# Two token tiles of a recurrence block share one matmul, ScalarE gathers the keys, and the output weights move into the mixer's weight buffers

## The chip, the cores and the metric

The kernel runs on one core of a Trainium2 chip. The metric is the device time of one launch in microseconds (us). The engines are TensorE (PE, with its weight loads as PEld), VectorE (DVE), ScalarE (ACT), GpSimd (POOL) and SyncE (SP), which issues most of the DMAs.

## The reference, cut to what matters

One layer of a hybrid encoder works on x, 2048 tokens of width 1024, in float32:

- A mixer: x += W_out [ DiffAttn(4 heads) || HGRN2(4 heads) ] (W_in RMSNorm(x)). The attention is causal by chunks of 64 tokens and takes the difference of two softmaxes. HGRN2 is a gated linear recurrence with 128 key and 128 value channels per head: within a chunk of 64 tokens, `att[t,s] = sum_k q[t,k] k[s,k] exp(b[t,k] - b[s,k])` for s <= t, where b is the running sum of the logarithms of the forget gates, and `o[t] = sum_s att[t,s] v[s] + (q exp(b)) state`; the state is carried from chunk to chunk.
- A feed-forward part: x += W_down (silu(conv3(u)) * v), with u and v from W_up RMSNorm(x).

## The kernel before, in words

The mixer runs over four heads `s`, and in a head over eight blocks `b` of 256 tokens, which are two token tiles of 128. For each head it loads the columns of W_in that the head needs, split into a high and a low half that are multiplied in three matmuls: `WA` (query, key, value of the attention), `WB` (value and gate of HGRN2), `WC` (query and forget gate of HGRN2). In a block, a string of letters gives the order in which the steps are written: projections (`A`, `B`, `I`, `J`, `C`) and transposes (`t`, `u`) of the next block, attention of this one (`a`, `b`, `x`, `y`), `h` for the recurrence within the block (`hgrn`), `k` for its output and state (`hgrn_o`). A compile-time scheduler turns what is written into one fixed queue for each engine; it mixes the steps by priority and by its own estimate of durations, and places all semaphores. Each engine works its queue off in order.

`hgrn` computes the matrix `att` of a tile in seven levels, h = 1, 2, 4, ... 64. At level h, the tokens are cut into runs of h; a run on the right side of a pair takes queries, the run on its left takes keys. For each of the block's two tiles one matmul (L441) multiplies the keys `kS` of the tile (128 - h columns as weights) with the 64 queries `qP` of the right-hand runs, and a masked copy (L444) on VectorE puts the result into the tile's `att`. Then VectorE multiplies the right-hand queries and the left-hand keys by the decay `T` of the neighbouring run (L449, L450) and shortens `T` by half (L452). The products of both tiles are made in one instruction. An f32 matmul shows as two records in the trace. `lt`, the result in PSUM, has one buffer, which it shares with `op` and `sp` of `hgrn_o`. `hgrn_o` multiplies `att` with the values, adds the part of the state, and renews the state (`sp`, L477).

The last stage of the first half, the output projection, holds W_out in eight tiles `wo`, of 128 rows each, with a high and a low half. Each is loaded to a buffer `raw`, cast by ScalarE (L537), and the low half is subtracted by GpSimd for even tiles and by VectorE for odd ones (L538). `wo` belongs to a pool that is opened after the mixer's pools are closed. For each token tile, `load_o` reads the mixer's output, transposes it on TensorE and splits it into `oT` (L555, L556); 48 matmuls `pjo` (L599 to L601) follow, and the residual, norm and transposes for the feed-forward part. That part (L619 on) isn't touched by the diff.

Of the kernel before, what the change touches and what calls it, by code (L numbers as in the profile page):

```python
# [18 lines left out]
P = 128  # L19
D = 1024  # L20
S = 2048
# [3 lines left out]
ROW = 512  # L25
TOP, FEW, SMALL, SMALL2 = 480, 192, 320, 192
FF = 2816
# [32 lines left out]


@with_exitstack
def hymba_kernel(ctx, tc, x, ln1_w, w_in, q_norm_w, k_norm_w, lam_q1, lam_k1, lam_q2, lam_k2,
                 diff_subln_w, hgrn_lb_logits, hgrn_norm_w, w_out, ln2_w, w_up, conv_w, conv_b,
                 w_down, out):
    nc = tc.nc
# [50 lines left out]
    hgw = cst.tile([P, P], F32, name="hgw")  # L117
    lmask = few.tile([P, 7, 64], U8, name="lmask")
    NATT = 3
    atts = [cst.tile([P, P], F32, name=f"att{n}") for n in range(NATT)]  # L120

# [13 lines left out]
    def load_rest(tmp, tmq):  # L135
        lamv = tmp[:, 0:256].rearrange("p (n e) -> p n e", n=4)
        lbd = tmp[:, 256:268].rearrange("p (n e) -> p n e", n=3)
        lmf = tmq[:, 0:448].rearrange("p (l e) -> p l e", l=7)
        for hf in range(2):
# [32 lines left out]
        POOL.tensor_copy(out=lmask, in_=lmf)  # L172
        for a in atts:
            POOL.memset(a, 0.0)
# [8 lines left out]


    with ExitStack() as ms:
        wp = pool(ms, "wp", 1)
        kv = pool(ms, "kv", KVB, side="right")
# [25 lines left out]
        def phase1(b):  # L213
# [42 lines left out]
        for s in range(4):  # L256
# [87 lines left out]
            def attn(b, j):  # L344
# [9 lines left out]
                for si, (k0, k1) in enumerate(segs):  # L354
                    for c in range(2):
# [71 lines left out]
            def hgrn(b):  # L427
                f, kS, qP, qk = HG.pop(b)
                T = f
                TT = wk.tile([P, BLK], F32, name="TT", tag="TT", bufs=FB)  # L430
                to = 0
                att = [atts[(2 * b + g) % NATT] for g in range(2)]
                for li, h in enumerate(LEVELS):
                    nb = BLK // (2 * h)
                    nk = P - h
                    lt = ps.tile([P, 2, 64], F32, name="lt", tag=HT, bufs=HB)
                    qv = qP.rearrange("p (n two h) -> p n two h", two=2, h=h)
                    kvw = kS.rearrange("p (n two h) -> p n two h", two=2, h=h)
# [9 lines left out]
                    Tv = T.rearrange("p (n two) -> p n two", two=2)  # L448
                    DVE.tensor_tensor(out=qv[:, :, 1, :], in0=qv[:, :, 1, :], in1=Tv[:, :, 0:1].broadcast_to([P, nb, h]), op=ALU.mult)  # L449
                    DVE.tensor_tensor(out=kvw[:, :, 0, :], in0=kvw[:, :, 0, :], in1=Tv[:, :, 1:2].broadcast_to([P, nb, h]), op=ALU.mult)  # L450
                    Tn = TT[:, to:to + nb]
                    DVE.tensor_tensor(out=Tn, in0=Tv[:, :, 0], in1=Tv[:, :, 1], op=ALU.mult)  # L452
                    T = Tn
                    to += nb
                HG[b] = (qk, kS, qP, T)

            def hgrn_o(b):
                qk, kS, qP, T = HG.pop(b)
                att = [atts[(2 * b + g) % NATT] for g in range(2)]
                for g in range(2):  # L460
# [61 lines left out]
    up_st = ExitStack()  # L522
    hp = pool(up_st, "hp3", 1, side="right")
    with ExitStack() as ms:
        wp = pool(ms, "wp2", 1)
# [5 lines left out]
        pa = pool(ms, "pa2", 2, space=PSUM, side="right")  # L531
        WO = []
        for kt in range(ND):
            raw = rw.tile([P, D], F32, name="raw", tag="raw")
            dma(out=raw, in_=w_out[kt * P:(kt + 1) * P, :])
            w = wp.tile([P, 2, D], F32R, name=f"wo{kt}")
            ACT.copy(w[:, 0], raw)  # L537
            (POOL if kt in WOP else DVE).tensor_tensor(out=w[:, 1], in0=raw, in1=w[:, 0].bitcast(F32), op=ALU.subtract)  # L538
            WO.append(w)

        OT = {}

        def load_o(i):
            ot = wk.tile([P, D], F32, name="ot", tag="ot")
            dma(out=ot, in_=o_d[i])
            xt = wk.tile([P, D], F32, name="xt", tag="xt", bufs=XTB)
            dma(out=xt, in_=x[i * P:(i + 1) * P, :])
            oT = [wk.tile([P, D], F32R, name="oT", tag=f"oT{a}", bufs=2) for a in range(2)]
            for hf in range(2):
                tp = pa.tile([P, 512], F32, name="tpo", tag="x")  # L550
                for q in range(4):
                    kt = hf * 4 + q
                    PE.transpose(tp[:, q * P:(q + 1) * P], ot[:, kt * P:(kt + 1) * P], ident)
                cs = slice(hf * 512, hf * 512 + 512)
                ACT.copy(oT[0][:, cs], tp)  # L555
                DVE.tensor_tensor(out=oT[1][:, cs], in0=tp, in1=oT[0][:, cs].bitcast(F32), op=ALU.subtract)  # L556
            OT[i] = (oT, xt)
# [319 lines left out]
HT, HB = "h", 1  # L877
WOP = (0, 2, 4, 6)
EARLY, TP, LO, HSB, HVB, XTB = 1, 1, 2, 5, 3, 2
LOPOOL = (6,)  # L880
# [28 lines left out]
```

## Time and profile before

| | us |
|---|---|
| median of 3 runs | 2762.63 |
| lowest and highest run | 2759.31, 2767.03 |
| the profiled execution | 2761.66 |
| its span in the trace | 2760.0 |
| PE busy | 2662.2 (96%) |
| DVE busy | 1892.9 (69%) |
| ACT busy | 1212.4 (44%) |
| POOL busy | 1053.6 (38%) |

The span is that of the profiled execution; busy times are sums of the instructions' durations without overlap within an engine. Matmuls are pipelined, so the duration of one is longer than what it takes of the queue: that is read from the distance of the starts.

### The profile page before, as it was taken

To read this page: it belongs to the slowest core of one execution; us is meant where nothing else is said; L and a number is where in the kernel's file an instruction comes from. 1 tells how busy PE (TensorE), PEld (TensorE's weight loads), DVE (VectorE), ACT (ScalarE), POOL (GpSimd) and SP (SyncE) were. 2 spreads that over 40 slices of the span, in tenths; PEclk is the share of its full clock that TensorE was granted. 3 is DMA by queue.
4 is the path that set the end of the run, shared out by engine and by line. 5 is a ranking of instruction groups with operands and counts; after the bars stand their busy time and mean duration, and the time that the engine had idled before them with its cause. 6 is when DMAs were issued, how large, how long until landed. Compare 5 with 4: busy or idle time off the path is not lost. (4 is left out here: it accounts for less than half of the span.)

```text
span 2760.0 us, 43193 instructions
## 1 busy us (share of the span) xinstructions
PE 2662.2 (96%) x15170; PEld 2329.6 (84%) x15170; DVE 1892.9 (69%) x4051; ACT 1212.4 (44%) x2878; POOL 1053.6 (38%) x1153
## 2 busy tenths in 40 slices
PE   7999999999999999989999999999999998899999
PEld 6888999999999999978877888887888886687887
DVE  4667855676667666773338666668777768978787
ACT  4555544454345444454335344345434434334332
POOL 2222222212222222220334443444344347877775
PEclk9999999999999999999999999999999999999999
DMA  5333422232222322125754232225222234775754
GB/s 183 119 109 112 130 89 86 82 124 83 99 83 75 115 91 84 50 88 172 248 192 142 83 92 75 86 92 175 77 85 91 70 92 129 170 159 132 178 172 168
DMA packets 273494, 322.96 MB, mean 117 GB/s; under 512 B 19470, under 2 KB 238974, under 8 KB 269182
## 3 DMA queue, kind: packets, MB, share of 16 engines
q1 hardware_dynamic: 266366, 295.04, 32.8%
q0 software_dynamic: 6912, 25.17, 5.3%
q8 instruction: 120, 1.97, 0.3%
q14 instruction: 96, 0.79, 0.1%
HBM read 198.50 MB, written 104.86 MB: 110 GB/s over the span
## 5 line engine op out<-in xcount | busy, mean ns | idle before, releaser
L684 PE MATMUL q<-xT,WS 128*128 128x512 f32 x704 | 274.4, 390 | 2.4 <-DVE xT L617 2.4
L683 PE MATMUL q<-xT,WS 128*128 128x512 f32 x704 | 274.4, 390 | 0.5 <-ACT xT L616 0.5
L685 PE MATMUL q<-xT,WS 128*128 128x512 f32 x704 | 274.3, 390 | 0.6 <-DVE WS L617 0.4
L797 PE MATMUL pd<-TW,SG 128*128 128x512 f32 x616 | 245.1, 399 | 21.2 <-DVE acc L803 7.1
L799 PE MATMUL pd<-TW,SG 128*128 128x512 f32 x616 | 243.2, 396 | 2.2 <-DVE SG L617 2.2
L798 PE MATMUL pd<-TW,SG 128*128 128x512 f32 x616 | 244.0, 397 | 0.5 <-DVE TW L617 0.5
L616 ACT CAST WS<-st 128x512 fp32r<-128x512 f32 x176 | 108.4, 618 | 243.6 <-PE q L685 227.1
L684 PE MATMUL q<-xB,WS 128*128 128x512 f32 x528 | 205.9, 390 | 2.2 <-DVE xB L617 2.2
L685 PE MATMUL q<-xB,WS 128*128 128x512 f32 x528 | 206.1, 390 | 1.2 <-DVE WS L617 1.2
L683 PE MATMUL q<-xB,WS 128*128 128x512 f32 x528 | 205.8, 390 | 0.7 <-ACT xB L616 0.7
L378 ACT ACTIVATE p<-sc,nm 128x1024 f32<-128x1024 f32 (+4 forms) x192 | 165.7, 863 | 90.3 <-DVE nm L367 87.5
L617 POOL TENSOR_TENSOR WS<-st,WS 128x512 fp32r<-128x512 f32 x44 | 88.2, 2004 | 278.4 <-ACT WS L616 258.8
L252 PE MATMUL pj<-WA,hT 128*128 128x384 f32 x512 | 176.4, 344 | 4.1 <-DVE hT L239 4.1
L367 DVE TENSOR_REDUCE nm<-sc 128x1 f32<-128x1024 f32 (+4 forms) x192 | 174.5, 909 | 6.9 <-PE sc L363 4.3
L253 PE MATMUL pj<-WA,hT 128*128 128x384 f32 x512 | 175.3, 342 | 0.0
L254 PE MATMUL pj<-WA,hT 128*128 128x384 f32 x512 | 174.5, 341 | 0.0
L797 PEld LDWEIGHTS pd<-TW,SG 128*128 128x128 f32 x616 | 118.1, 192 | 52.1 <-DVE acc L803 7.6
L684 PEld LDWEIGHTS q<-xT,WS 128*128 128x128 f32 x704 | 132.3, 188 | 30.4 <-DVE xT L617 3.1
L685 PEld LDWEIGHTS q<-xT,WS 128*128 128x128 f32 x704 | 132.3, 188 | 29.0 <-DVE WS L617 1.4
L683 PEld LDWEIGHTS q<-xT,WS 128*128 128x128 f32 x704 | 132.4, 188 | 28.6 <-ACT xT L616 0.9
L616 ACT CAST WS<-rawu 128x512 fp32r<-128x512 f32 x132 | 82.0, 623 | 159.2 <-PE q L685 159.2
L252 PE MATMUL pjc<-hT,WC 128*128 128x256 f32 x512 | 151.6, 296 | 0.2 <-ACT ig L321 0.2
(412 smaller groups left out, 7857.3 us busy)
## 6 DMA issues: line engine op xcount, KB each, us to landing
hT<-hTd SPq DMA_DIRECT2D x24, 2048.0 KB, 7.9
rawu<-in_w_up_dram SPq DMA_DIRECT2D x176, 256.0 KB, 3.1
x2d<-acc POOLq DMA_DIRECT2D x48, 512.0 KB, 6.5
gd<-c SPq DMA_DIRECT2D x176, 128.0 KB, 1.8
G<-gd SPq DMA_DIRECT2D x24, 768.0 KB, 4.2
xt<-in_x_dram SPq DMA_DIRECT2D x32, 512.0 KB, 4.1
hTd<-hT SPq DMA_DIRECT2D x8, 2048.0 KB, 6.2
qT<-qh SPq DMA_DIRECT2D x256, 64.0 KB, 2.0
```

The costliest lines, as they stand in the source:

```text
L252: PE.matmul(dst, lhsT=lh, rhs=rh, start=dt == 0, stop=False)
L253: PE.matmul(dst, lhsT=lh, rhs=rl, start=False, stop=False)
L254: PE.matmul(dst, lhsT=ll, rhs=rh, start=False, stop=dt == ND - 1)
L367: DVE.tensor_reduce(out=nm, in_=sc[:, 0:w], axis=AX.X, op=ALU.max, negate=True)
L378: ACT.activation(out=p[:, 0:w], in_=sc[:, 0:w], func=AF.Exp, bias=nm, accum_out=l)
L616: ACT.copy(dst[:, 0], src)
L683: PE.matmul(dst, lhsT=w[:, 0, cs], rhs=b_[:, 0, dt], start=dt == 0, stop=False)
L684: PE.matmul(dst, lhsT=w[:, 0, cs], rhs=b_[:, 1, dt], start=False, stop=False)
L685: PE.matmul(dst, lhsT=w[:, 1, cs], rhs=b_[:, 0, dt], start=False, stop=dt == 3)
L797: PE.matmul(pd, lhsT=Sx[n][:, 0, k], rhs=w[:, 0], start=k == 0, stop=False)
L798: PE.matmul(pd, lhsT=Sx[n][:, 0, k], rhs=w[:, 1], start=False, stop=False)
L799: PE.matmul(pd, lhsT=Sx[n][:, 1, k], rhs=w[:, 0], start=False, stop=k == len(qs) - 1)
```

## The change

Four parts:

- **Token order.** A second input `xm` is handed over, x in tiles of 128 tokens with the tokens of every odd tile in reversed order. The mixer reads its tokens from `xm`, and so works on odd tiles back to front: the recurrence's runs have the queries on the left and the keys on the right there, and the attention's mask of the last 128 keys covers the other 64 rows. The output stage reads `oT` of odd tiles back to front, so that the rest sees the usual order; the residual is read from `x` as before.
- **Shared matmuls.** At a level, the left-hand keys of the even tile and the right-hand keys of the odd tile stand at places that complement each other. A copy gathers the 64 keys of each into `kp`, 128 columns, and one matmul multiplies `kp` with the 128 queries of both tiles. Two quadrants of the result are used, by the same two masked copies, with a mask for each tile order. The copy is made by ScalarE, in the very last block of the last head by VectorE.
- **Buffers.** The masks (twice as many) and `att` (four buffers, two for each tile of a block, where there were three in rotation) move from the constants into a pool of the mixer; `kp` has two buffers.
- **Output weights.** The pool of `WA`, `WB` and `WC` lives until the output stage ends. In the last head, after the last block's projection `B`, tiles 0 to 2 of W_out are prepared in the buffer of `WA`; after `J`, tiles 3 and 4 in that of `WB`; after `C`, tiles 5 and 6 in that of `WC`. Tile 7 is prepared in the output stage.

```diff
+def view(a, off, *dims):
+    return bass.AP(a.tensor, a.offset + off, [list(a.ap[0])] + [list(d) for d in dims if d[1] > 1])
...
-        for li, h in enumerate(LEVELS):
-            v = lmf[:, li, :].rearrange("p (n h) -> p n h", h=h)
-            n = 64 // h
-            for pat, base, mul in (([-2 * h, n], 0, 1), ([2 * h, n], h - 1, -1)):
-                POOL.affine_select(out=v, in_=v, pattern=[pat, [0, h]], compare_op=ALU.is_ge,
-                                   fill=0.0, base=base, channel_multiplier=mul)
+        for g in range(2):
+            for li, h in enumerate(LEVELS):
+                v = lmf[:, g, li, :].rearrange("p (n h) -> p n h", h=h)
+                n = 64 // h
+                for pat, base, mul in (([-2 * h, n], -g * h, 1), ([2 * h, n], h - 1 + g * h, -1)):
+                    POOL.affine_select(out=v, in_=v, pattern=[pat, [0, h]], compare_op=ALU.is_ge,
+                                       fill=0.0, base=base, channel_multiplier=mul)
...
+    def prep_wo(w, kt):
+        raw = rw.tile([P, D], F32, name="raw", tag="raw")
+        dma(out=raw, in_=w_out[kt * P:(kt + 1) * P, :])
+        ACT.copy(w[:, 0], raw)
+        (POOL if kt in WOP else DVE).tensor_tensor(out=w[:, 1], in0=raw, in1=w[:, 0].bitcast(F32), op=ALU.subtract)
+        WO.append(w)
...
-                dma(out=xt, in_=x[b * BLK + j * P:b * BLK + (j + 1) * P, :])
+                dma(out=xt, in_=xm[2 * b + j])
...
-                            DVE.memset(sc[0:64, w - 64:w], -3.0e38)
+                            if j:
+                                DVE.memset(sc[64:P, w - P:w - 64], -3.0e38)
+                            else:
+                                DVE.memset(sc[0:64, w - 64:w], -3.0e38)
...
-                att = [atts[(2 * b + g) % NATT] for g in range(2)]
+                att = [atts[g][b % 2] for g in range(2)]
                 for li, h in enumerate(LEVELS):
-                    nb = BLK // (2 * h)
-                    nk = P - h
+                    n, m = 64 // h, P // h
+                    qv = view(qP, h, (P - h, 2), (2 * h, n), (1, h))
+                    kl = view(kS, 0, (2 * h, n), (P + h, 2), (1, h))
+                    kf = view(kS, 0, (P + h, 2), (2 * h, n), (1, h))
                     lt = ps.tile([P, 2, 64], F32, name="lt", tag=HT, bufs=HB)
-                    qv = qP.rearrange("p (n two h) -> p n two h", two=2, h=h)
-                    kvw = kS.rearrange("p (n two h) -> p n two h", two=2, h=h)
-                    for g in range(2):
-                        ng = nb // 2
-                        PE.matmul(lt[0:nk, g].rearrange("p (n h) -> p n h", h=h), lhsT=kS[:, g * P:g * P + nk],
-                                  rhs=qv[:, g * ng:(g + 1) * ng, 1, :], start=True, stop=True)
+                    kp = wk.tile([P, P], F32, name="kp", tag="kp", bufs=2)
+                    kd = view(kp, 0, (2 * h, n), (h, 2), (1, h))
+                    if s == 3 and b == NB - 1:
+                        DVE.tensor_copy(out=kd, in_=kl)
+                    else:
+                        ACT.copy(kd, kl)
+                    PE.matmul(view(lt, 0, (64, 2), (h, n), (1, h)), lhsT=kp, rhs=qv, start=True, stop=True)
                     for g in range(2):
                         DVE.copy_predicated(
-                            out=att[g][0:nk].rearrange("p (n two h) -> p n two h", two=2, h=h)[:, :, 1, :],
-                            mask=lmask[0:nk, li].rearrange("p (n h) -> p n h", h=h),
-                            data=lt[0:nk, g].rearrange("p (n h) -> p n h", h=h))
+                            out=att[g].rearrange("p (n two h) -> p n two h", two=2, h=h)[:, :, 1 - g, :],
+                            mask=lmask[:, g, li].rearrange("p (n h) -> p n h", h=h),
+                            data=lt[:, g].rearrange("p (n h) -> p n h", h=h))
...
+                    DVE.tensor_tensor(out=qv, in0=qv, in1=view(T, 0, (m + 1, 2), (2, n), (0, h)), op=ALU.mult)
+                    DVE.tensor_tensor(out=kf, in0=kf, in1=view(T, 1, (m - 1, 2), (2, n), (0, h)), op=ALU.mult)
...
                     if nb_ < NB:
                         step[c_](nb_)
+                        if s == 3 and nb_ == NB - 1 and c_ in WOS:
+                            k0, n, tg = WOS[c_]
+                            wt = wp.tile([P, n, 2, D], F32R, name=f"wo{tg}", tag=tg)
+                            for k in range(n):
+                                prep_wo(wt[:, k], k0 + k)
...
+        prep_wo(wp.tile([P, 2, D], F32R, name="wo7"), 7)
...
+                if i % 2:
+                    tv = tv[:, :, ::-1]
+                ACT.copy(oh, tv)
+                DVE.tensor_tensor(out=ol, in0=tv, in1=oh.bitcast(F32), op=ALU.subtract)
...
+WOS = {"B": (0, 3, "WA"), "J": (3, 2, "WB"), "C": (5, 2, "WC")}
```

## Rows read from the trace of the kernel before

**Rows 1.** Busy time of each engine by stretch, with granted clock (1.00 is 2.4 GHz).

```profile
320.00:613.00 293.00, 287.12 (x2109) 271.27 (x2107) 194.60 (x663) 135.76 (x405) 66.28 (x127) 1.00 0.27 87
...
1190.00:1252.00 62.00, 51.04 (x325) 44.30 (x324) 45.97 (x105) 31.32 (x71) 17.03 (x20) 0.92 0.34 110
1252.00:1450.00 198.00, 193.53 (x965) 161.53 (x964) 63.77 (x89) 74.53 (x194) 49.41 (x61) 1.00 0.64 208
```

**Rows 2.** Waits of PE, 320 to 1190 us: total us, times, longest.

```profile
PE av L416 <- ACT aT L413: 2.2, 8, 0.7
...
PE lt L441 <- DVE kS L450: 0.8, 3, 0.3
```

**Rows 3.** PE in order of time, level h=1: start us, us, instruction.

```profile
621.43 0.56 PE L441 MATMUL lt<-qP,kS 128*127 128x64 f32 x4
...
622.05 0.34 PE L253 MATMUL pj<-WA,hT 128*128 128x384 f32 x1
622.23 0.34 PE L254 MATMUL pj<-WA,hT 128*128 128x384 f32 x1
```

**Rows 4.** The same view, level h=32.

```profile
632.47 0.47 PE L441 MATMUL lt<-qP,kS 128*96 128x64 f32 x4
...
632.95 0.28 PE L253 MATMUL pj<-WB,hT 128*128 128x256 f32 x1
633.07 0.28 PE L254 MATMUL pj<-WB,hT 128*128 128x256 f32 x1
```

**Rows 5.** The same view, level h=64.

```profile
635.71 0.28 PE L252 MATMUL pj<-WB,hT 128*128 128x256 f32 x1
635.92 0.45 PE L441 MATMUL lt<-qP,kS 128*64 128x64 f32 x4
...
636.52 0.28 PE L254 MATMUL pj<-WB,hT 128*128 128x256 f32 x1
```

**Rows 6.** PE in order of time around one matmul of the state.

```profile
1160.66 0.38 PE L477 MATMUL sp<-ig,kt__15685 128*128 128x128 f32 x2
...
1161.06 0.33 PE L252 MATMUL pj<-WA,hT 128*128 128x384 f32 x1
```

**Rows 7.** ACT in order of time, a copy of 128 x 128.

```profile
1154.12 0.29 ACT L473 COPY kt__15662<-op 128x128 f32<-128x128 f32 x1
```

**Rows 8.** Groups of ACT, 320 to 1190 us: count, busy us, mean ns, idle before.

```profile
L413 ACT COPY aT<-tpa 128x512 f32<-128x512 f32 (+2 forms) x118 | 58.3, 518 | 26.1 <-PE tpa L411 25.7
```

**Rows 9.** PE in order of time at the seam, [idle before <- released by].

```profile
1208.92 0.61 PE L477 MATMUL sp<-ig,kt__16242 128*128 128x128 f32 x2 [3.29 <-ACT op L485]
...
1214.60 1.11 PE L441 MATMUL lt<-qP,kS 128*126 128x64 f32 x4 [3.51 <-DVE kS L450]
...
1217.80 0.77 PE L599 MATMUL pjo<-wo,oT 128*128 128x512 f32 x1
```

**Rows 10.** DVE in order of time at the seam.

```profile
1204.47 2.31 DVE L423 SCALAR_TENSOR_TENSOR fo<-ro_r,r 128x1 f32<-128x1 f32 x1 [1.44 <-POOL ro_r L100]
...
1210.38 2.42 DVE L487 SCALAR_TENSOR_TENSOR o<-o,rh_r,sg 128x128 f32<-128x128 f32 x1 [0.46 <-POOL rh_r L100]
```

**Rows 11.** POOL in order of time at the seam.

```profile
1204.40 2.36 POOL L538 TENSOR_TENSOR wo<-raw,wo 128x1024 fp32r<-128x1024 f32 x1
...
1210.32 2.34 POOL L538 TENSOR_TENSOR wo<-raw,wo 128x1024 fp32r<-128x1024 f32 x1
```

**Rows 12.** ACT in order of time, the first cast of an output weight.

```profile
1192.92 1.04 ACT L537 CAST wo<-raw 128x1024 fp32r<-128x1024 f32 x1
```

**Rows 13.** PE in order of time, the last matmul that reads WA.

```profile
1169.35 0.33 PE L254 MATMUL pj<-WA,hT 128*128 128x384 f32 x1
```

**Rows 14.** POOL in order of time before the first block.

```profile
18.58 6.03 POOL L170 TENSOR_SCALAR_AFFINE_SELECT tmq<-tmq 128x64 f32<-128x64 f32 x14
...
29.80 0.61 POOL L290 TENSOR_TENSOR qn<-qr,rq_r 128x256 f32<-128x256 f32 x1
```

**Rows 15.** PE in order of time, the first transposes of query and key.

```profile
34.74 0.38 PE L299 MATMUL tpq<-ident,qn 128*128 128x128 f32 x2
```

More of the change, by code (lines that the diff above doesn't have):

```diff
@@ L25 @@
 ROW = 512
-TOP, FEW, SMALL, SMALL2 = 480, 192, 320, 192
+TOP, FEW, SMALL, SMALL2 = 480, 128, 320, 192
 FF = 2816
@@ L64, in hymba_kernel @@
                  diff_subln_w, hgrn_lb_logits, hgrn_norm_w, w_out, ln2_w, w_up, conv_w, conv_b,
-                 w_down, out):
+                 w_down, xm, out):
     nc = tc.nc
@@ L117, in hymba_kernel @@
     hgw = cst.tile([P, P], F32, name="hgw")
-    lmask = few.tile([P, 7, 64], U8, name="lmask")
-    NATT = 3
-    atts = [cst.tile([P, P], F32, name=f"att{n}") for n in range(NATT)]
     def load_ln1(tp):
@@ L165, in load_rest @@
         POOL.memset(lmf, 1.0)
-        for li, h in enumerate(LEVELS):
-            v = lmf[:, li, :].rearrange("p (n h) -> p n h", h=h)
-            n = 64 // h
-            for pat, base, mul in (([-2 * h, n], 0, 1), ([2 * h, n], h - 1, -1)):
-                POOL.affine_select(out=v, in_=v, pattern=[pat, [0, h]], compare_op=ALU.is_ge,
-                                   fill=0.0, base=base, channel_multiplier=mul)
-        POOL.tensor_copy(out=lmask, in_=lmf)
-        for a in atts:
+        for g in range(2):
[5 more added lines that the diff above has]
+                                       fill=0.0, base=base, channel_multiplier=mul)
+        POOL.tensor_copy(out=lmask[:, :, 0:7], in_=lmf)
+        for a in atts[0] + atts[1]:
             POOL.memset(a, 0.0)
@@ L182, in hymba_kernel @@
     rw = pool(ctx, "rw", RB)
+    up_st = ExitStack()
+    out_st = ExitStack()
+    wp = pool(out_st, "wp", 1)
+    WO = []
+    def prep_wo(w, kt):
[4 more added lines that the diff above has]
+        WO.append(w)
     with ExitStack() as ms:
-        wp = pool(ms, "wp", 1)
+        mc = pool(ms, "mc", 1, side="right")
+        lmask = mc.tile([P, 2, 8, 64], U8, name="lmask")
+        atts = [[mc.tile([P, P], F32, name=f"att{g}{n}") for n in range(2)] for g in range(2)]
         kv = pool(ms, "kv", KVB, side="right")
@@ L453, in hgrn @@
+                    DVE.tensor_tensor(out=kf, in0=kf, in1=view(T, 1, (m - 1, 2), (2, n), (0, h)), op=ALU.mult)
+                    Tn = TT[:, to:to + m]
+                    DVE.tensor_tensor(out=Tn, in0=view(T, 0, (2, m)), in1=view(T, 1, (2, m)), op=ALU.mult)
                     T = Tn
-                    to += nb
+                    to += m
                 HG[b] = (qk, kS, qP, T)
@@ L458, in hgrn_o @@
                 qk, kS, qP, T = HG.pop(b)
-                att = [atts[(2 * b + g) % NATT] for g in range(2)]
+                att = [atts[g][b % 2] for g in range(2)]
                 for g in range(2):
@@ L519, in hymba_kernel @@
                         step[c_](nb_)
-    up_st = ExitStack()
+                        if s == 3 and nb_ == NB - 1 and c_ in WOS:
[3 more added lines that the diff above has]
+                                prep_wo(wt[:, k], k0 + k)
     hp = pool(up_st, "hp3", 1, side="right")
-    with ExitStack() as ms:
+    with out_st as ms:
         wp = pool(ms, "wp2", 1)
@@ L531, in hymba_kernel @@
         pa = pool(ms, "pa2", 2, space=PSUM, side="right")
[L532 to L539, printed above, removed]
+        prep_wo(wp.tile([P, 2, D], F32R, name="wo7"), 7)
         OT = {}
@@ L553, in load_o @@
                     PE.transpose(tp[:, q * P:(q + 1) * P], ot[:, kt * P:(kt + 1) * P], ident)
-                cs = slice(hf * 512, hf * 512 + 512)
-                ACT.copy(oT[0][:, cs], tp)
-                DVE.tensor_tensor(out=oT[1][:, cs], in0=tp, in1=oT[0][:, cs].bitcast(F32), op=ALU.subtract)
+                tv, (oh, ol) = tp.rearrange("p (q c) -> p q c", c=P), [
+                    t[:, hf * 512:hf * 512 + 512].rearrange("p (q c) -> p q c", c=P) for t in oT]
+                if i % 2:
+                    tv = tv[:, :, ::-1]
+                ACT.copy(oh, tv)
+                DVE.tensor_tensor(out=ol, in0=tv, in1=oh.bitcast(F32), op=ALU.subtract)
             OT[i] = (oT, xt)
@@ L903 @@
         args.append(nc.dram_tensor(f"in_{name}_dram", a.shape, mybir.dt.from_np(a.dtype), kind="ExternalInput").ap())
+    xm = np.array(inputs["x"]).reshape(S // P, P, D)
+    xm[1::2] = xm[1::2, ::-1]
+    arrays["in_xm_dram"] = xm
+    args.append(nc.dram_tensor("in_xm_dram", xm.shape, F32, kind="ExternalInput").ap())
     args.append(nc.dram_tensor("out_0_dram", (1, S, D), F32, kind="ExternalOutput").ap())
```

7 lines of the change are left out of this document (1 added, 6 removed).

## The prediction

> **What bounds the kernel now.** I read the busy times by stretch first, then the waits of TensorE, then the instructions in order of time around the three places that the diff touches. In a head of the mixer, TensorE is busy for 287.12 of 293.00 us, VectorE for 194.60 and ScalarE for 135.76 [rows 1]: the stage runs at TensorE's pace, and a microsecond taken out of its queue is a microsecond of the end as long as the next instruction in that queue is ready. It mostly is: in the 870 us of heads 1 to 3 the level matmuls `lt` waited 0.8 us for the keys in all, and the `av` matmuls, which get their operand from a ScalarE copy, waited 2.2 us [rows 2]. The order of the queues is laid out ahead of the run, so a longer chain is met by a later place in the queue and not by a stall, if the planner sees the length rightly. The exception is the seam between mixer and output projection: there TensorE is busy for 51.04 of 62.00 us, at a mean granted clock of 0.92 [rows 1]. After it the output stage is TensorE's again (193.53 of 198.00 us, ScalarE 74.53, VectorE 63.77) [rows 1], and the feed-forward stages, untouched by the diff, hold the rest.
>
> **The shared level matmuls: minus 43.6 us.** Per block and level, two f32 matmuls of 64 columns, one for each token tile (four records), become one of 128 columns (two records). What a group costs the queue is the time from its start to the start of the second instruction behind it, less that instruction's usual spacing, because the first one behind it is held up too. Level h=1: 622.05 - 621.43 = 0.62, less 0.18 (622.23 - 622.05), gives 0.44 [rows 3]. Level h=32: 632.95 - 632.47 = 0.48, less 0.12, gives 0.36 [rows 4]. The levels between get narrower weights step by step, so I take the mean of the two ends, 0.40, for six levels. Level h=64 also holds up what stands before it: 636.52 - 635.71 = 0.81, less two spacings of 0.12, gives 0.57 [rows 5]. Together 6 x 0.40 + 0.57 = 2.97 us for a block. No row shows the new matmul itself. The nearest is `sp`, one f32 matmul of 128 columns on 128 x 128 weights between two projection matmuls: 1161.06 - 1160.66 = 0.40, less 0.18, gives 0.22 [rows 6]. Seven of these are 1.54 us, so 1.43 us a block are saved. There are 32 blocks (4 heads of 8); the last one runs in the seam, where TensorE waits anyway, so 31 count: 44 us, or 43.6 with the spacings unrounded. From both sides: `sp` streams adjacent columns and the new matmul strided ones from two tiles, so the cost could lie anywhere between 0.22 and what the pair costs today, 0.40, and the term between 0 and 44. I take 0.22, since the pair already streams strided columns and its cost falls with the width of the weights (0.44 to 0.36 for 127 to 96 columns, 64 streamed in both), which speaks for the weights as what is paid for.
>
> The Trainium skill (TensorE: Matmul & The Clock Gate, section on LDWEIGHTS) states that a weight load takes its number of columns divided by 1.2, in ns. By that alone, as an estimate, a block's 4 x 769 columns of today and 14 x 128 of the change differ by 1.07 us, 33 us in 31 blocks. The fall from 0.44 to 0.36 [rows 3, 4] agrees with it, the 0.57 of the narrowest weights does not; what the time is if it holds for all levels is rival 1.
>
> **The mixed keys on ScalarE: plus 4 us.** Before each level matmul a copy `kp` gathers 64 keys of each tile: 7 x 32 - 7 = 217 copies, 128 x 128. A ScalarE copy of that size took 0.29 [rows 7], so some 62 us of work go to an engine that is idle for half of the stage (135.76 of 293.00) [rows 1]; that work costs nothing by itself. What costs is the wait. The chain of a level was key product on VectorE, matmul, masked copy on VectorE; it becomes key product, copy, matmul, masked copy. The copy stands in ScalarE's queue until VectorE is done, and behind it stand the exponentials and the `aT` copies, for which the next score matmuls and `av` wait. The nearest row is the existing hand-over from a ScalarE copy to TensorE: 2.2 us over 118 `aT` copies [rows 2, 8], 0.019 each, or 4 us for 217. Below it the bound is 0; above it, if no matmul found a later place, 217 x 0.29 = 62 us. I take 4, because the planner's places for the present chain were off by only 0.8 us.
>
> **The output weights: minus 9 us.** The eight f32 weight tiles are split by a ScalarE cast and a subtraction on GpSimd (even tiles) or VectorE. The first cast stands at 1192.92 [rows 12], though the buffer under it was read last at 1169.35 by WA's final matmul [rows 13]. So all eight fall into the seam, and no `pjo` matmul can fill TensorE until 1217.80 [rows 9]. The change hands out the buffers as WA, WB and WC are read for the last time: tiles 0 to 2 some 23 us sooner, 3 and 4 after WB, 5 and 6 as now, 7 as now. Two of the seam's waits end in this work: 3.29 us for `sp` and 3.51 us for the level h=2 [rows 9]. Behind the first VectorE needed 2.31 us for a 128 x 1 product, behind the second 2.42 us for a 128 x 128 one [rows 10], each while GpSimd subtracted a weight tile (2.36 and 2.34 us) [rows 11]. That is 6.8 us. The clock adds to it: a mean of 0.92, with levels of 2.4 and 1.2 GHz, is some 10 us at the lower, and a level group there took 1.11 against 0.56 [rows 3, 9]; some 4 of these 10 us are the waits, 6 are work at half speed, 3 us lost. 9.8 in all; I take 9, because tile 6 still is subtracted by GpSimd in the seam. Bounds: 0, and all idle time plus the clock, 11 + 3 = 14.
>
> What speaks against the move: the two long VectorE instructions lie beside two subtractions on GpSimd [rows 10, 11], and three such subtractions of 2.4 us move into the body of the last head; if TensorE waited there as in the seam, 7 us would come back (rival 5). I expect little of it, as projection matmuls stand ready there. The Trainium skill (SBUF — State Buffer, "Who interferes with whom") states the cause as a rule: a VectorE instruction with two SBUF inputs is blocked for the whole of a GpSimd instruction that reads SBUF. The rows agree with it.
>
> **What I cost at nothing.** The masks for two tile orders: 14 more selects on GpSimd before the first block. Fourteen took 6.03 us; 6 more would push the query scaling that ended at 30.41 to some 34 by the order of that queue [rows 14], and its transpose starts at 34.74 [rows 15]; without that cover it is 2 to 3 us, once. The reversed reads when the output stage splits `oT`: that stage has ScalarE idle for 123 of 198 us [rows 1], so even a doubled cost stays covered. The masked rows of the score tile, the products on strided views and the residual loads keep number and size. The attention mask, `att` with four buffers instead of three, and the moved pools issue nothing more. In the last block the copy is VectorE's, seven products' worth, 2 us in the seam, within the bounds given there.
>
> **The sum.** 2761.66 (the profiled execution, 2760.0 of it span; the median is 1 us higher) - 43.6 + 4 - 9 = 2713.
>
> **The rivals.** (1) Only the weights are paid for. Then level h=64 costs today what half of the width of h=1 costs, 0.22 and not 0.57, and the rest of its row is a pause that another instruction will make; a block saves 6 x 0.40 + 0.22 - 1.54 = 1.08 us, 33 us in all: 2761.7 - 33 + 4 - 9 = 2724. For it: the fall with width [rows 3, 4]; against it: [rows 5]. The skill's estimate above, from a weight load's columns, comes to the same time. (2) The strided 128 columns cost more than `sp`. Half-way to today's pair, 0.31 a level, saves 2.97 - 2.17 = 0.8 us a block, 25 us: 2732. For it: no row has such a matmul; against it: 64 streamed columns in each of six levels, and yet a cost that follows the width of the weights. (3) The hop takes back half: a copy that lands 0.1 us late at each level holds the queue for 22 us, and lengthens the seam by 4: 2761.7 - 43.6 + 22 - 5 = 2735. For it: ScalarE serves in order and an exponential of 1024 columns can stand in front; against it: [rows 2]. (4) Slower: the level matmuls keep their places and each waits for the whole copy, 217 x 0.29 = 62 us: 2761.7 - 43.6 + 62 - 9 = 2771. It decides from (43.6 + 9) / 217 = 0.24 us a level. Against it: both kinds of wait in [rows 2] are 3 us together. (5) The seam's gain is lost: the last block's softmax and recurrence set its length anyway (2722), or the moved subtractions block VectorE in the last head, 3 x 2.4 = 7 us (2720). For it: VectorE is busy for 45.97 of its 62 us [rows 1]; against it: the two blocked instructions there.
>
> **How the numbers follow.** The forecast, 2698 to 2719, has a chance of 0.45; rival 1 0.12, rival 2 0.11, rival 3 0.11, rival 4 0.08, rival 5 0.07, and 0.06 is left for a gain beyond 2698, should a group hold up more neighbours than I counted. The likeliest time is 2713. The range reaches from just under the forecast's lower end to past rival 3, with rival 2's and 3's own spread: 2695 to 2746. A change under 0.3% (8 us) is about what a measurement here cannot tell from none. Faster are the forecast, rivals 1, 2, 3 and 5 and the rest, less the far ends of rivals 2 and 3: 0.87; same, those ends and a part of rival 4: 0.05; slower 0.08.
>
> **What the profile after would show.** Level matmuls in two records, some 450 in all, with a cost of 0.22 by the same reading; TensorE busy some 11 us less in a head, and heads of 282 us. ScalarE copies of 0.3 us, 217 of them, and a wait of `lt` for `kp` of a few us in all. Casts of the output weights from about 1170, `pjo` matmuls before 1200 by the old clock, and the two waits of over 3 us gone. Wrong would be: heads as long as now, with TensorE waiting for `kp`; level matmuls that cost 0.3 or more; or new waits of VectorE on GpSimd in the last head.

## The result, and the profile after

The changed kernel takes 2784.51 us (median of 4 runs, 2778.73 to 2786.75) against 2762.65 before: a ratio of 1.0076, 95% interval 1.0063 to 1.0088. It is 22 us slower, where 2713 was predicted, and the profiled execution (2784.47, span 2782.5) shows that two quite separate things happened.

The matmuls went: TensorE has 14722 instructions instead of 15170. The first view is the busy time of each engine in the stretches of [rows 1], now of the changed kernel: the stretch and its length, the busy us of TensorE, its weight loads, VectorE, ScalarE and GpSimd (instructions in brackets), the granted clock, the share of the DMA engines, GB/s.

```profile
320.00:613.00 293.00, 282.80 (x2018) 264.24 (x2017) 198.23 (x668) 153.70 (x470) 65.73 (x130) 1.00 0.29 96
1190.00:1252.00 62.00, 40.65 (x209) 33.99 (x210) 33.17 (x98) 22.40 (x58) 9.55 (x15) 0.73 0.10 31
1252.00:1450.00 198.00, 192.75 (x941) 160.74 (x942) 60.31 (x83) 69.26 (x178) 36.01 (x49) 0.96 0.61 199
```

In the body of a head TensorE is idle for 10.2 of 293 us instead of 5.9. At the seam it is busy for 40.65 of 62 us, where it was 51.04, at a mean granted clock of 0.73, where it was 0.92, and the DMA engines, at a share of 0.34 before, are nearly empty at 0.10. The stage that should fill this stretch is missing. The same stretch in order of time, TensorE first and SyncE's queue below it:

```profile
1233.99 0.79 PE L499 MATMUL sp<-ig,kt__16855 128*128 128x128 f32 x2 [1.58 <-ACT op L507]
...
1243.53 2.05 PE L436 MATMUL av<-vst,aT 128*128 128x128 f32 x16 [0.24 <-ACT aT L433]
1251.90 1.97 PE L572 MATMUL tpo<-ident,ot 128*128 128x128 f32 x8 [6.32 <-DMA ot<-od]
1254.42 0.79 PE L621 MATMUL pjo<-woWA,oT 128*128 128x512 f32 x1 [0.55 <-DVE oT L578]
1255.01 0.63 PE L622 MATMUL pjo<-woWA,oT 128*128 128x512 f32 x1
1255.44 0.63 PE L623 MATMUL pjo<-woWA,oT 128*128 128x512 f32 x1
...
1465.88 0.39 PE L623 MATMUL pjo<-wo,oT 128*128 128x512 f32 x1
```

```profile
1231.71 5.78 SPq L510 DMA_DIRECT2D od<-o  x2
1247.65 0.32 SPq L445 DMA_DIRECT2D od<-oo  x1
1248.02 0.42 SPq L564 DMA_DIRECT2D ot<-od  x1
```

The rows of the kernel before that these answer to, SyncE's and TensorE's:

```profile
1189.70 0.43 SPq L545 DMA_DIRECT2D ot<-od  x1
```

```profile
1250.00 0.39 PE L477 MATMUL sp<-ig,kt__16581 128*128 128x128 f32 x2
...
1441.86 0.39 PE L601 MATMUL pjo<-wo,oT 128*128 128x512 f32 x1
```

The mixer ends sooner than before: its last `sp` stands at 1233.99, before at 1250.00. But the first `pjo` comes at 1254.42 instead of 1217.80 [rows 9]. It waits for `tpo`, that waits 6.32 us for the load of `ot`, and this load is issued only behind the mixer's very last store (1247.65); before, it was issued at 1189.70, with the last block still under way. So no projection work stands between the last block's softmax and recurrence steps, TensorE runs dry, and the granted clock falls with it: the first `pjo` matmuls are 0.43 us apart (1255.01, 1255.44), at the lower of the two levels (1.2 GHz), against 0.23 further on (1259.97 to 1260.20), at the full one (2.4 GHz). The last `pjo` comes at 1465.88 instead of 1441.86. That is 24 us, a little more than the whole loss of 22.

The steps of the mixer, by the readings of [rows 3] and [rows 5], level h=1 and level h=64 of one block:

```profile
620.47 0.39 PE L465 MATMUL lt<-qP,kp 128*128 128x128 f32 x2
620.61 0.43 PE L270 MATMUL pj<-WA,hT 128*128 128x384 f32 x1
620.88 0.34 PE L271 MATMUL pj<-WA,hT 128*128 128x384 f32 x1
...
633.89 0.28 PE L271 MATMUL pj<-WB,hT 128*128 128x256 f32 x1
634.08 0.46 PE L465 MATMUL lt<-qP,kp 128*128 128x128 f32 x2
634.29 0.36 PE L269 MATMUL pj<-WB,hT 128*128 128x256 f32 x1
634.49 0.28 PE L270 MATMUL pj<-WB,hT 128*128 128x256 f32 x1
```

Level h=1 costs 620.88 - 620.47 - 0.18 = 0.23, against 0.44 before; the prediction had 0.22. Level h=64 costs 634.49 - 633.89 - 2 x 0.12 = 0.36, against 0.57. Over the groups of heads 1 to 3 that stand between three projection matmuls without a recorded wait (from 3 groups at h=1, 2 and 8 to 20 at h=64), the seven levels cost 0.22, 0.22, 0.36, 0.22, 0.23, 0.30 and 0.31, some 1.9 us a block; by the same count the kernel before pays 3.1. So some 1.25 us a block are saved, 38 to 39 us in 31 blocks. Yet the last projection matmul of the mixer (`pjc`) starts only 4 us sooner (1188.36 instead of 1192.32). What took its place is partly in the waits of TensorE, as in [rows 2] (320 to 1190 us: total, times, longest):

```profile
PE op L487 <- DVE st L504: 6.7, 11, 0.8
PE av L436 <- ACT aT L433: 4.0, 7, 1.4
PE lt L465 <- DVE qP L471: 4.0, 7, 2.3
```

`av` waited 2.2 before, and `lt` 0.8. The longest of these waits, 2.3 us, lies in the last head. The next fence shows it in order of time on GpSimd, VectorE and TensorE:

```profile
1169.69 2.40 POOL L197 TENSOR_TENSOR woWA<-raw,woWA 128x1024 fp32r<-128x1024 f32 x1
...
1170.33 1.92 DVE L471 TENSOR_TENSOR qP<-qP,f 128x128 f32<-128x128 f32 x1
...
1172.39 0.47 PE L465 MATMUL lt<-qP,kp 128*128 128x128 f32 x2 [2.34 <-DVE qP L471]
```

The query product, 0.29 us in other levels (the next one stands at 1173.38), took 1.92 beside a weight subtraction on GpSimd, as the two VectorE instructions of [rows 10] took over 2.3 beside those of [rows 11].

### The profile page after: what moved, and what is told of

It reads as the page before. It is cut to its first block, busy times and chain, and to the rows that moved or that the text cites. A ratio compares the mean times of both kernels' runs of the same rounds, so it can differ in the third digit from the quotient of the medians.

```text
span 2782.5 us, 42697 instructions
## 1 busy us (share of the span) xinstructions
PE 2651.1 (95%) x14722; PEld 2303.3 (83%) x14722; DVE 1900.4 (68%) x4058; ACT 1262.0 (45%) x3095; POOL 1053.8 (38%) x1168
## 3 DMA queue, kind: packets, MB, share of 16 engines
q8 instruction: 117, 1.92, 0.3%
## 5 line engine op out<-in xcount | busy, mean ns | idle before, releaser
L436 PE MATMUL av<-vst,aT 128*128 128x128 f32 x1088 | 152.7, 282 | 8.2 <-ACT aT L433 7.8
```

## Experiments

**What holds the output stage back.** The diff moves pools, the address ranges from which a stage takes its tiles in SBUF. The mixer's right-hand side grows by 4096 bytes a partition (`lmask` 1024, four `att` 2048, two `kp` 1024), and the left-hand side shrinks by 2048 (`lmask` 448 and `att` 1536 go, and a pad of 64). In the layouts of the compiled programs, in bytes of a partition:

```
                                  before             after
output stage, pool wk2      103424 - 136192    101376 - 134144
  of it the tile ht         132096 - 136192    130048 - 134144
mixer, pool sm, begins at            137536             133440
mixer, pools hp and pp       98304 - 137216     94208 - 133120
```

`sm` holds the small softmax tiles that live to the end of the last block. Before, `wk2` overlapped only `hp` and `pp`, which are done early. Theory M: the 704 bytes that the end of `wk2` now shares with `sm` hold back the whole pool. Rival Q: the stage waits for its weights, or stands behind something else in the DMA queue.

First run, the changed kernel with `ht` taken out of `wk2`:

```
         wk = pool(ms, "wk2", 1)
+        wh = pool(ms, "wh2", 1)
...
-            ht = wk.tile([P, D], F32, name="ht", tag="ht")
+            ht = wh.tile([P, D], F32, name="ht", tag="ht")
```

> The changed kernel with one thing more: the output stage's tile ht gets a pool of its own, at the same address, so that the pool of the stage's other tiles (ot, xt, oT) ends at byte 130048 of a partition instead of 134144, below the mixer's pool of small softmax tiles that begins at 133440. Nothing else moves. Theory M (the stage is held out of the mixer's last block because the two pools overlap): first pjo back from 1254 to 1205-1220 us, the half clock behind 1200 mostly gone, 2750 to 2762 us. Rival Q (it is held out by its weights, now prepared in the last head, or by the order of the DMA queue): first pjo stays near 1254, 2784 us within 3.

Measured: 2755.36 us (12 runs), ratio to before 0.9974, interval 0.9965 to 0.9984; 29 us below the changed kernel. This kernel is called the split kernel from here on. Its profiled execution (2747.18 us, the fastest of its runs), by stretch, and its first `pjo`:

```profile
1190.00:1252.00 62.00, 55.16 (x308) 47.31 (x307) 33.78 (x92) 23.91 (x62) 5.92 (x16) 0.92 0.19 63
1252.00:1450.00 198.00, 192.26 (x951) 160.15 (x950) 70.54 (x92) 79.09 (x197) 57.04 (x64) 0.99 0.66 214
```

```profile
1195.15 0.80 PE L622 MATMUL pjo<-woWA,oT 128*128 128x512 f32 x1 [2.35 <-DVE oT L579]
1195.75 0.63 PE L379 MATMUL sc<-kst,qT 128*128 128x512 f32 x1
```

The first `pjo` is back among the last block's score matmuls, sooner than the 1205 to 1220 expected, and TensorE is busy for 55.16 of the 62 us. The tile `ht` still lies on the same bytes. So it was not the bytes of `ot`, `xt` or `oT` that collided: the pool was held back as a whole by what its last tile overlapped.

Second run, the converse: the kernel before, with 2048 unused bytes at the top of the mixer's side.

```
-        kv = pool(ms, "kv", KVB, side="right")
+        pool(ms, "padp", 1, side="right").tile([P, 512], F32, name="padt"); kv = pool(ms, "kv", KVB, side="right")
```

> The kernel before with 2048 unused bytes a partition at the top of the mixer's side, so that its pool of small softmax tiles begins at 135488 and overlaps the output stage's pool (103424 to 136192) by 704 bytes, as in the changed kernel. The instructions are the same. Theory M: the first pjo goes from 1217.8 to 1260-1275 us (behind the mixer's last store) and the time rises by 15 to 30 us, to 2778-2792. Rival Q: the time stays within 3 us of 2762.

Measured: 2788.23 us (5 runs), ratio 1.0093, interval 1.0081 to 1.0105. A kernel with the same instructions becomes 26 us slower by unused memory. By stretch, and in order of time, it repeats the seam of the changed kernel:

```profile
1190.00:1252.00 62.00, 41.02 (x231) 34.89 (x228) 39.77 (x93) 27.80 (x64) 17.23 (x18) 0.75 0.20 58
```

```profile
1256.34 1.97 PE L553 MATMUL tpo<-ident,ot 128*128 128x128 f32 x8 [6.25 <-DMA ot<-od]
1258.86 0.79 PE L599 MATMUL pjo<-wo,oT 128*128 128x512 f32 x1 [0.55 <-DVE oT L556]
```

Both runs bear theory M out, and Q falls. The second run also puts the stage's small tiles (`sm2`) into the range of `sm`, where they lie in the changed and the split kernel too; the last run below takes them out.

**The two halves of the change.** Third run: the split kernel with the output weights prepared in the output stage, as before (eight tiles in `wp2`, the call of `prep_wo` in the last head gone, the pool of `WA`, `WB` and `WC` closed with the mixer).

> The changed kernel with the split of the first experiment and the output weights prepared in the output stage as before (eight tiles of their own): the recurrence's shared matmuls alone. If the prediction's step for the weights holds (-9 us), this is 9 us above the split kernel; if the GpSimd subtractions in the last head cost VectorE as much as they save, it is within 3 us of it. Against before: the four heads gave back all but 4 us of the 33 us of PE time saved, so 2752 to 2760; by the prediction's own sum 2720.

Measured: 2759.27 us (11 runs), ratio 0.9986, interval 0.9976 to 0.9996. The shared matmuls alone are worth 3.4 us, where the prediction's terms for them, -43.6 and +4, say 39.6. Against the first run, the weights are worth 3.9, between the 9 and the 3 that were expected; the two intervals overlap.

Fourth run: the kernel before with only the weights moved into the last head (`prep_wo`, the longer life of the pool and tile 7 as in the change; of the edit only the call is shown).

```
...
+                        if s == 3 and nb_ == NB - 1 and c_ in WOS:
+                            k0, n, tg = WOS[c_]
+                            wt = wp.tile([P, n, 2, D], F32R, name=f"wo{tg}", tag=tg)
+                            for k in range(n):
+                                prep_wo(wt[:, k], k0 + k)
...
```

> The kernel before with only the output weights moved into the last head (layout of memory as before, so nothing is held out). By the prediction's step: 2753 to 2756 (-9, -6 at least). Rival (GpSimd's four subtractions of 2.4 us block VectorE in the last head while the recurrence waits for it, and the seam was covered by attention anyway): 2761 to 2768.

Measured: 2762.95 us (11 runs), ratio 1.0006, interval 0.9997 to 1.0014: no gain, as its rival expected. The two stretches around WA's last use, of this kernel:

```profile
1150.00:1200.00 50.00, 45.22 (x313) 41.43 (x312) 38.51 (x94) 27.16 (x66) 16.85 (x19) 0.97 0.28 80
1200.00:1252.00 52.00, 45.55 (x272) 38.79 (x271) 35.17 (x96) 23.75 (x61) 10.32 (x15) 0.90 0.24 79
```

and of the kernel before:

```profile
1150.00:1200.00 50.00, 49.41 (x367) 46.31 (x366) 36.49 (x105) 26.97 (x74) 11.27 (x17) 1.00 0.18 54
1200.00:1252.00 52.00, 41.60 (x255) 35.82 (x254) 37.86 (x90) 24.80 (x56) 14.64 (x19) 0.90 0.29 94
```

The seam gains 3.95 us of TensorE's work, and the 50 us ahead of it lose 4.19. The hole has moved.

**Does GpSimd dig that hole?** Two runs put all eight weight subtractions on VectorE (`WOP = ()`), one in the split kernel, one in the fourth run's.

> The split kernel with all eight subtractions for the output weights on VectorE, none on GpSimd. In the last head the waits of TensorE were 10.5 us against 4.7 before, with the longest beside GpSimd's subtractions of 2.4 us. If these block VectorE: 3 to 5 us faster, 2750 to 2752. If the loss is the work's own place in VectorE's queue: no faster, 2754 to 2760.

> The kernel of the fourth experiment (before, with only the output weights moved into the last head; it gained nothing) with all eight weight subtractions on VectorE. If GpSimd's subtractions in the last head are what took the gain of the earlier weights: 4 to 8 us faster than before, 2755 to 2759. If the preparation's work merely takes the last head's time in place of the seam's, whichever engine does it: 2760 to 2765.

Measured: 2753.56 us (5 runs), 0.9965 (0.9953 to 0.9978), and 2759.94 us (11 runs), 0.9992 (0.9983 to 1.0001): 1.8 and 3.0 us below their counterparts. Both times fall between the two ranges that were expected, and each pair of intervals overlaps; that both moved the same way speaks for some 2 to 3 us, but does not show them. What the trace shows is the last 41 us ahead of the last `pjc` (1181.4 in the split kernel, 1186.8 in the one without GpSimd's subtractions), first of the split kernel:

```profile
1140.00:1181.00 41.00, 36.38 (x255) 33.71 (x254) 32.84 (x82) 23.51 (x60) 17.75 (x19) 1.00 0.29 83
```

```profile
1146.00:1187.00 41.00, 39.35 (x281) 36.75 (x280) 32.90 (x95) 25.49 (x69) 10.74 (x16) 1.00 0.29 85
```

GpSimd is busy for 7.0 us less, VectorE, which now does the subtractions, for no longer than before, and TensorE gets 3.0 us back. As wholes, the two profiled executions (2747.18 and 2749.42 us) do not show that gain. The Trainium skill (SBUF — State Buffer, "Who interferes with whom") states that a VectorE instruction with two SBUF inputs contends with a GpSimd instruction that reads SBUF. The product of 1.92 us beside the subtraction of 2.40, against 0.29 alone, agrees with it.

**Where the matmuls' saving went.** Three theories: the hop by ScalarE takes it back (H); what TensorE saves turns into waits and pauses elsewhere, with nothing added (W); TensorE's time is the bound and the additions took it back (P). Fifth run, the purest test: the kernel before with the second tile's matmul left out.

```
-                    for g in range(2):
+                    for g in range(1):
                         ng = nb // 2
...
-                            data=lt[0:nk, g].rearrange("p (n h) -> p n h", h=h))
+                            data=lt[0:nk, 0].rearrange("p (n h) -> p n h", h=h))
```

> The kernel before with the second token tile's recurrence matmuls left out (its masked copies read the first tile's scores, so its part of the output is not computed): TensorE loses about as much work as in the change, and nothing is added: no copy of keys, the same shapes on VectorE, the same memory. Theory P (TensorE's time is the bound and the change's additions took the saving back): 33 to 37 us go, 2726 to 2732. Theory W (TensorE's saving turns into waits for VectorE's chain wherever the next work is not ready): half or less of it goes, 2745 to 2755.

Measured: 2748.22 us (5 runs), ratio 0.9949, interval 0.9936 to 0.9961. A level group costs it 1.97 us a block by the count above, 36 us saved in 31 blocks, and only 14.4 arrive. The stretches are cut at the start of each head's first projection matmul, at the last `pjc` and at the last `pjo`; first the kernel before, then this one:

```profile
21.00:315.00 294.00, 279.17 (x2010) 263.48 (x2011) 200.54 (x659) 155.13 (x439) 76.33 (x154) 0.99 0.37 127
315.00:608.00 293.00, 287.81 (x2119) 272.25 (x2118) 193.92 (x663) 137.03 (x409) 67.64 (x128) 1.00 0.27 88
608.00:902.00 294.00, 288.12 (x2122) 272.81 (x2121) 196.78 (x666) 137.78 (x410) 66.12 (x128) 1.00 0.29 93
902.00:1192.00 290.00, 284.98 (x2104) 270.42 (x2104) 192.13 (x661) 131.02 (x400) 65.93 (x128) 1.00 0.25 83
1192.00:1441.00 249.00, 236.73 (x1249) 199.34 (x1248) 102.33 (x180) 102.21 (x256) 61.28 (x75) 0.98 0.57 184
```

```profile
21.00:316.00 295.00, 276.47 (x1913) 258.60 (x1912) 199.50 (x659) 155.59 (x439) 74.10 (x153) 0.97 0.37 127
316.00:602.00 286.00, 278.95 (x2006) 261.25 (x2005) 193.54 (x662) 136.80 (x408) 65.31 (x128) 1.00 0.27 90
602.00:888.00 286.00, 279.37 (x2008) 261.45 (x2007) 195.87 (x665) 138.06 (x409) 68.74 (x128) 1.00 0.29 95
888.00:1172.00 284.00, 277.24 (x1991) 259.62 (x1990) 192.91 (x661) 132.50 (x401) 69.04 (x128) 1.00 0.26 84
1172.00:1429.00 257.00, 239.74 (x1241) 200.64 (x1241) 103.12 (x181) 102.27 (x256) 63.39 (x76) 0.97 0.55 180
```

Heads 1 to 3 are 6 to 8 us shorter each, some 20 in all. Head 0, which also normalises and transposes its input, is 1 us longer: the idle time of TensorE rises from 14.8 to 18.5 us, and its mean clock falls from 0.99 to 0.97. The stretch from the last `pjc` to the last `pjo` is 7 us longer (unrounded, 1192.32 to 1441.86 before and 1172.79 to 1429.14 now). It holds the last block's chain, which the saving does not shorten, and now TensorE waits 2.7 and 2.3 us for VectorE ahead of two `tph` groups, where it waited 1.1 before. So 22 of the 36 us do not arrive although nothing was added: P falls.

The rows say where they went. TensorE's idle time rises by 13 us: 3.7 in head 0, 4.4 in heads 1 to 3 and 5.0 in the last stretch. The rest is the granted clock. Three stretches of head 0, each at a mean of 1.00 in the kernel before, stand like this now:

```profile
110.00:120.00 10.00, 8.25 (x55) 7.78 (x55) 7.28 (x23) 6.68 (x22) 1.65 (x5) 0.83 0.05 15
190.00:200.00 10.00, 9.11 (x46) 8.32 (x47) 6.82 (x21) 5.11 (x15) 0.74 (x2) 0.83 0.35 141
280.00:290.00 10.00, 10.00 (x53) 9.81 (x53) 5.28 (x16) 3.96 (x15) 0.74 (x2) 0.83 0.58 232
```

In each, or just ahead of it, TensorE had waited: 1.26 and 1.92 us for VectorE's `hT`, and 2.26 us for ScalarE's `p`. The kernel before is idle for about as long in two of these stretches (busy for 8.40 and 8.35 of 10 us) and keeps the full clock there, so what decides is not shown. The whole execution has a mean clock of 0.988, the profiled one of the kernel before 0.992, and all five runs of this kernel lie at 0.987 to 0.989, those of the kernel before beside them at 0.990 to 0.993. With levels of 2.4 and 1.2 GHz, 0.004 of 2748 us is, as an estimate from these means, 11 us of work lost to the lower level. 13 and 11 make up the 24 us by which the profiled execution, 12 us shorter in span, misses the 36. So W stands in part: the saving turned into idle time at three places, and nearly as much into time at the lower clock, which no theory had named.

Sixth run: the split kernel without the copy of the keys (the first tile's keys are the weights; the buffers of `kp` stay, so that the layout does).

```
-                    kp = wk.tile([P, P], F32, name="kp", tag="kp", bufs=2)
-                    kd = view(kp, 0, (2 * h, n), (h, 2), (1, h))
-                    if s == 3 and b == NB - 1:
-                        DVE.tensor_copy(out=kd, in_=kl)
-                    else:
-                        ACT.copy(kd, kl)
-                    PE.matmul(view(lt, 0, (64, 2), (h, n), (1, h)), lhsT=kp, rhs=qv, start=True, stop=True)
+                    if s == 0 and b == 0: DVE.memset(wk.tile([P, P], F32, name="kp", tag="kp", bufs=2), 0.0)
+                    PE.matmul(view(lt, 0, (64, 2), (h, n), (1, h)), lhsT=kS[:, 0:P], rhs=qv, start=True, stop=True)
```

> The split kernel with the copy of the mixed keys left out: the shared matmul takes the first tile's 128 keys in place as its weights (so the recurrence's scores are wrong for the second tile). No hop by ScalarE, none of its 51 us of copies between 320 and 1180 us. Theory H (the hop takes the saving back): 15 to 22 us faster than the split kernel, 2733 to 2740. Theory W: 2 to 6 us faster, 2749 to 2753; what remains of the loss is in waits for VectorE and in held-up neighbours.

Measured: 2751.46 us (5 runs), ratio 0.9956, interval 0.9943 to 0.9968: 3.9 us below the split kernel, though the two intervals just overlap. H falls: the hop does not take 15 to 22 us.

Seventh run: the split kernel with every copy of the keys on VectorE (`DVE.tensor_copy(out=kd, in_=kl)` alone).

> The split kernel with the mixed keys copied by VectorE in every block, not only the last (0.21 us there against 0.31 on ScalarE, and no change of engine in the chain). Theory H: the waits for the copy and for aT and p on ScalarE go, 5 to 12 us faster, 2743 to 2750. Theory W: VectorE is what the recurrence and the softmax wait for already and gets 200 copies more (some 42 us of work): 0 to 10 us slower, 2755 to 2765.

Measured: 2761.39 us (11 runs), ratio 0.9993, interval 0.9984 to 1.0002: 6.0 us above the split kernel. W's reading of VectorE (194.60 of 293.00 us busy in [rows 1]) as the engine that has no room to give passes this test, but the clock is a rival here too: the eleven runs have a mean granted clock of 0.988 to 0.992, the split kernel's twelve 0.989 to 0.994. What share of the 6 us it has is not shown.

The reading fails the next test. Last of these, the fifth run's kernel with the second tile's masked copies left out too (`for g in range(1)` ahead of `copy_predicated`), so that VectorE loses 55 us of work.

> The kernel of the fifth experiment (before without the second tile's recurrence matmuls, 2748) with the second tile's masked copies left out too: 224 copies of 0.25 us, some 55 us of VectorE's work. If what TensorE saved was lost in waits for VectorE's queue: 8 to 20 us faster than the fifth, 2728 to 2740, so that nearly the whole saving is paid. If it was lost elsewhere (the clock, ScalarE's softmax, the seam): 2744 to 2750.

Measured: 2760.89 us (11 runs), ratio 0.9991, interval 0.9982 to 1.0000. Not 8 to 20 us faster: 12.7 slower than with that work. Its first two heads, and the largest wait of TensorE from 20 to 320 us:

```profile
21.00:321.00 300.00, 278.72 (x1912) 261.33 (x1911) 194.48 (x610) 154.82 (x439) 78.86 (x154) 0.96 0.36 123
321.00:614.00 293.00, 282.99 (x2007) 263.85 (x2007) 188.30 (x607) 137.04 (x409) 67.06 (x128) 0.99 0.27 90
```

```profile
PE sc L362 <- ACT p L378: 7.5, 6, 2.3
```

and the same wait in the fifth run:

```profile
PE sc L362 <- ACT p L378: 2.3, 1, 2.3
```

VectorE is busy for 5 us less in each, and each is 5 to 7 us longer than in the fifth run: TensorE is idle for some 3 us more in each, and the mean clock is lower by 0.01 in each, which is some 3 us again. TensorE waits 7.5 us in head 0 for ScalarE's exponentials to free the score tile, where it waited 2.3. The order of each queue is planned anew for every edit, and this plan puts score matmuls where the softmax is not yet done. That a freer VectorE brings the saving home is not borne out, and it is not ruled out for another plan. Whether the other order alone makes the 12.7 us is not shown, since no run here holds the order fixed while an instruction goes. The same holds for the differences of 2 to 6 us between other pairs of kernels here.

**A version that beats both.** The changed kernel with the split, `WOP = ()`, and the output stage's small tiles allocated ahead of its large ones:

```
         wp = pool(ms, "wp2", 1)
-        wk = pool(ms, "wk2", 1)
         sm = pool(ms, "sm2", 4)
         sm.small([P, SMALL2 // 4], F32, name="pad", bufs=1)
+        wk = pool(ms, "wk2", 1)
+        wh = pool(ms, "wh2", 1)
```

> The changed kernel with the tile ht in a pool of its own, no weight subtraction on GpSimd, and the output stage's small tiles allocated ahead of its large ones, so that of the stage's pools only that of ht overlaps the mixer's small softmax tiles. If those small tiles held the stage's first token tile back: 2746 to 2751. If not: as the split kernel without GpSimd, 2751 to 2756. Either way faster than both kernels.

Measured: 2747.78 us (5 runs, 2747.27 to 2750.61), ratio 0.9953, interval 0.9940 to 0.9967. It beats before by 15 us and the changed kernel by 37. It lies in the range for the case that the small tiles held the stage back, 5.8 us below the run with the old order of the pools (2753.56), but the two intervals overlap and the two profiled executions are alike (2749.67 and 2749.42 us), so that cause is not shown.

## Why the prediction was wrong

The forecast lay 71 us below the result. The runs divide that up, each part as the difference of two kernels and so to within a few us: 29 us are the held-back output stage (2784.51 - 2755.36), 36 the shared matmuls (39.6 predicted for the matmuls and the hop together, 3.4 paid), 5 the output weights (9 predicted, 3.9 paid behind the shared matmuls, nothing in the fourth run); the rest is the 1 us between the profiled execution and the median.

- **"The moved pools issue nothing more."** This is the step that turned the sign. They do issue nothing more, but they decide when another stage may be issued. The sum took the seam as it stood and improved it by 9; in fact the stage that filled it from 1198 on went behind the mixer's end. The rival on the slower side had the wrong mechanism: it put the loss at the hop, 62 us of waits for `kp`, and the waits for ScalarE's `kp` come to 2.6 us in the whole kernel.
- **The shared matmuls, minus 43.6.** The cost of one was right where the nearest row resembled it (0.23 against 0.22 at h=1), and too low at h=4, 32 and 64 (0.30 to 0.36): some 38 us are saved by the same reading, not 44, between the forecast and rival 1. What failed is the step after it, "a microsecond taken out of its queue is a microsecond of the end as long as the next instruction in that queue is ready". The fifth run takes 36 us out with nothing added, and 14 arrive. [rows 2] showed small waits, and I read them as room to spare. With less work between, 13 us of idle time open, and some 11 us (an estimate) go to the lower clock, which the sum priced at the seam alone. That the waits were small because the plan had filled TensorE to the point where the next operands were just ready is my reading; no run shows it. I also priced head 0 like the other heads and left the last block's seam out; the fifth run gains nothing in the one and loses 7 us in the other. The change gets 11 us less than the fifth run (3.4 against 14.4): 3.9 of them are the copy's by the sixth run, the rest stays open.
- **The hop, plus 4.** Right in its mechanism, a wait of a few us: `lt` waits 2.6 us for ScalarE's copy in the changed kernel. That the sixth run's difference, 3.9, hits the number is in part luck, since its plan differs too and the intervals overlap.
- **The output weights, minus 9.** The casts came even sooner than predicted (from 1162.43), and the seam gained, 4 us of work in the fourth run. But the stretch ahead of it lost 4.2, against "projection matmuls stand ready there". It is rival 5's place and mechanism in part, and the sign that was named for it, new waits of VectorE on GpSimd in the last head, came. The two runs without GpSimd's subtractions speak for some 2 to 3 us of it; that the rest is VectorE's and ScalarE's own added work is argued, not shown.
- **The masks, at nothing.** Right so far as it shows: 28 selects took 10.12 us in the changed kernel, and the first query scaling ended at 31.77, ahead of the old transpose at 34.74 [rows 15].

## What to carry to other kernels

When an edit resizes a pool, write down the byte ranges of the pools on both sides of the next stage's boundary, before costing any instruction: a new overlap with a pool that lives to the end held the whole next pool back here, and the cure was as small as giving one tile a pool of its own. Where one engine is 98% busy and its waits are small, an instruction saved is worth its full time only as far as what stands behind it is ready, and the granted clock of the stretches has to be compared along with the waits; the cheap test is to leave the instruction out altogether and see how much arrives, before the additions are weighed. A stretch with idle time is worth filling only if what fills it does not come from a stretch that was full.

## What the runs showed that was not expected

- 2048 unused bytes a partition cost 26 us (2762.63 to 2788.23), with the same instructions.
- Of 36 us of TensorE's work taken out with nothing added, 14 arrived; the mean granted clock of the runs was 0.987 to 0.989, where it was 0.990 to 0.993.
- Taking 55 us of VectorE's work out of a kernel made it 12.7 us slower (2748.22 to 2760.89).
- The product of 128 x 128 on VectorE took 1.92 us beside a GpSimd subtraction of 2.40, against 0.29, and TensorE waited 2.34 us for it; but with all eight subtractions on VectorE the time fell only by 1.8 and 3.0 us.
